# Four edits to the order of a one-core hybrid block: the S5 input's layout in DRAM, alternating layer-norm steps, the column-5 loads shared by up and down, and seven PSUM banks in the feed-forward

## The chip, the cores and the metric

One core of a Trainium2 chip runs the whole program. The metric is device microseconds of one execution; of the kernel before there are three runs, and their median is 1347.21 us (1343.9 to 1354.2). The engines are PE (matrix products), DVE (vector), ACT (activation), POOL (GpSimd) and SP (which issues nearly all the DMA loads of weights).

## What is computed

One layer on 256 latent and 256 context tokens of width 2048, batch 1. Cut to what matters here:

```python
m_lat = split(silu(c) @ w_ada + b_ada, 6)         # 2048 x 12288: six columns, each a vector of 2048
pl = split_in(modulate(x, m_lat[0], m_lat[1]) @ w_in)       # and pc, the same of ctx with m_ctx
ya = s5_mixer(pc[0], pl[0], ...)                  # 32 groups of 16 channels, 64 complex states, 2 directions
yd = mamba2_mixer(...)                            # bidirectional SSD
mix = concat([ya, chunk_gating(...), pool_mixer(...), yd]) @ w_out
h = layer_norm(ALPHA * x + m_lat[2] * mix, ln1_g, ln1_b)                      # "LN1" below
gate, val = split(modulate(h, m_lat[3], m_lat[4]) @ w_up, 2)                  # 2048 x 2*5632, "up"
f = (gelu(conv3x3(gate) + conv_b) * val) @ w_down                             # 5632 x 2048, "down"
out = layer_norm(ALPHA * h + m_lat[5] * f, ln2_g, ln2_b)                      # m_lat[5] is "column 5"
```

All weights are float32. Every large product is split into a high and a low part that the PE takes at a faster rate than float32.

## The kernel before, in words

Tokens lie along the free dimension (256 wide) and channels on the 128 partitions, so a vector of 2048 channels is 16 tiles (KT). A weight block of 128 x 1024 float32 (512 KB) is loaded by `load`, whose DMA stands on L158 and is issued by SP into one of a few buffers (`raw`, `pre`, `rxa`, `w`). `split` (L170 to L174) makes of each half of it a high part `wh` on ACT (L172) and a low part `wl` on DVE (L173), and `mm3` issues the matching pair of products on PE (L186 with `wh`, L187 with `wl`). DVE work outside this goes through the helpers `tt` (L202), `ts` (L197) and the scale-add on L205, so many different steps share these lines. A scheduler fixes the order of each engine's queue at build time from the order of the code, from priorities (`tc.high_priority`) and from dependencies; `yield` in the side work (a Python generator that `pump` advances between products) says how much PE time a piece stands for.

**Stages.** (1) 0 to 250 us: the six columns' products, interleaved with the input projection (`pA`, `bank`, L926). In it, four finished blocks of 128 S5 channels `pA[0..3]` are copied in time-reversed and straight form to `ut`, two buffers in turn, by two ACT copies each, and written to a DRAM tile `dU` (L968). The side work reads them back as `U` with 8 DMAs (L494), one for every eighth of the sequence, and makes from it 128 products `pS` in 8 steps (L503), each with `yield 3.4`; ACT copies them to `Z`, and a scan over `Z` follows on DVE (`wk<-Z,tab`, L202). (2) 250 to 438 us: the rest of the projection, the scan and the mixers, with products in between. (3) 438 to 565 us: the output projection `po`. (4) 565 to 596 us: LN1. `ln_stats` (L1137 to L1149) sums columns on PE, makes the mean, then the variance, its square root on ACT (L1147) and the reciprocal on DVE (L1148), and broadcasts both by products into two PSUM banks (L1149, `lsb`). Nine tiles or pairs then get `dT - mean` ("SU", L1217) and `dT * rstd` ("MU", L1218), both by `tt`, and ACT makes `hm` of each (L1220). The first two blocks of up (`NUP` = 2) are float32 products straight from `hm` and the raw weights, the two accumulators in turn (L1239). (5) 595 to 1091 us: up, 44 steps of `f`, each with two `half_up` (accumulator `pu`), a convolution on DVE and ACT (`cv`, `both`), and from `f` = 4 on one step of `gemv5`: one column-5 block of 512 KB loaded and accumulated on DVE (`acc<-raw,sc,acc`, 128 x 1024, L205), 32 blocks in all. (6) 1091 to 1338 us: down, 16 accumulators `pdn`, each with 44 K-tiles loaded in six blocks, and `ln_acc` after each. (7) the tail: `ln_stats` once more, SU and MU in pairs (L1350, L1351), scale and shift on ACT (L1340), store by SP (L1345).

**Banks.** PSUM tiles have tags: "main" with NMAIN = 3 banks and "side" with 4, the rest of the eight for `pg`. `pu`, `pdn`, `lst` (sums) and `lsb` take "main" in turn; `bank(name, tag)` may name another.

Of the kernel before, what the change touches and what calls it, by code (L numbers as in the profile page):

```python
# [51 lines left out]
def prep(i):  # L52
# [15 lines left out]
    wi = np.asarray(i["w_in"])[0]  # L68
    w1 = pm(np.concatenate([wi[:, :512], wi[:, 2560:2816]], 1))
    wt = pm(wi[:, :3584]).reshape(2, 8, P, 28, P).transpose(3, 0, 2, 1, 4).reshape(28, 2, P, 1024)  # L70
# [51 lines left out]
def build(tc, A, out, dbg=None):  # L122
# [41 lines left out]
    def wtile(n):  # L164
# [3 lines left out]
        return pool.tile([P, w], F32R, tag=tag, name="wh" if n == 0 else "wl", bufs=bufs)  # L168

    def split(src, n=512):  # L170
        h, l = wtile(0), wtile(1)
        S.copy(h[:, :n], src)  # L172
        V.tensor_sub(out=l[:, :n], in0=src, in1=h[:, :n])  # L173
        return h, l  # L174
# [141 lines left out]
    def side_gen():  # L316
# [175 lines left out]
        U = M.tile([P, G5, 64], F32, tag="U", name="U")  # L492
        for q in range(8):
            (GP, SY, (GP, SY)[q % 2])[BR].dma_start(out=U[q * 16:(q + 1) * 16], in_=G_["dU"].rearrange("(g h) q c -> h q g c", h=16)[:, q])  # L494

        Sth = [Z[:, n * 2048:n * 2048 + 2048].rearrange("p (c g k) -> p c g k", c=2, g=16) for n in range(2)]
        for e in range(8):
# [9 lines left out]
            for c_ in range(2):  # L507
                S.copy(St[hi, c_, g].rearrange("p g (s k) -> p g s k", s=2),
                       pv[hi, c_].rearrange("p g (s k) -> p g s k", s=2)[:, :, :, ::-1])
            yield 3.4  # L510

# [436 lines left out]
    for kp in range(8):  # L948
# [181 lines left out]
    def ln_stats(a12, s2_):  # L1130
# [11 lines left out]
        for n in range(4):  # L1142
            if n == 2:
                stt(st[:, 4:6], st[:, 0:2], -1.0, st[:, 0:2], MU, MU)
                tt(st[:, 4:6], st[:, 4:6], st[:, 2:4], AD)
                ts(st[:, 4:6], st[:, 4:6], 0.0, ALU.max)
                S.activation(out=st[:, 4:6], in_=st[:, 4:6], func=AF.Sqrt, bias=eps[:, 0:1])  # L1147
                V.reciprocal(out=st[:, 2:4], in_=st[:, 4:6])  # L1148
            PE.matmul(pb[n // 2][:, (n % 2) * P:(n % 2 + 1) * P], lhsT=st[:, n:n + 1].to_broadcast([P, P]), rhs=ident, start=True, stop=True)  # L1149
        return pb[0][:, :T], pb[1][:, :T]  # L1150

# [49 lines left out]
    for n in range(2):  # L1201
        rings[n][:] = [(wp, ("wh", "wl")[n], W_BUFS, 512), (fp, ("wh", "wl")[n], W_BUFS, 512)]
    mean, rstd = ln_stats(a12, s2l)
    gm = lnp.tile([P, 4, KT], F32, name="gm")
# [7 lines left out]
    hm = spare[0][:, 0:4096].rearrange("p (k t) -> p k t", k=KT)  # L1212
    raws += [spare[0][:, 4096:5120], spare[0][:, 5120:6144], spare[1][:, 0:1024], spare[1][:, 1024:2048]][:NSP]
    for c0, c1 in [(0, 1), (1, 2)] + [(ct, ct + 2) for ct in range(2, KT, 2)]:
        d = dT[:, c0:c1]
        bc = lambda a: a.unsqueeze(1).to_broadcast([P, c1 - c0, T])
        tt(d, d, bc(mean), SU)  # L1217
        tt(d, d, bc(rstd), MU)  # L1218
        for ct in range(c0, c1):
            S.activation(out=hm[:, ct], in_=dT[:, ct], func=AF.Identity, scale=gm[:, 0, ct:ct + 1],  # L1220
                         bias=gm[:, 1, ct:ct + 1])


# [51 lines left out]
    for f in range(FT):  # L1275
        if f >= G5S:
            next(g5, None)
# [28 lines left out]
        if FT - KT <= f:  # L1306
# [3 lines left out]
                             bias=gm[:, 3, ct:ct + 1]))  # L1310
    for _ in g5:
        pass


    b12 = lnp.tile([P, 2, T], F32, tag="a12", name="b12")
    shg = lnp.tile([P, T], F32, tag="shf", name="shg")
    for ct in range(KT):
# [11 lines left out]
        s2l = ln_acc(ct, pt, mm[:, 3], dT[:, ct], b12, shg)  # L1329
        if ct == 0:  # L1330
            sqrt_table()
    mean, rstd = ln_stats(b12, s2l)
    rm = fp.tile([P, 2, T], F32, tag="hm", name="rm", bufs=1)
# [69 lines left out]
```

## Time and profile before

| | us |
|---|---|
| median of 3 runs | 1347.21 (1343.9 to 1354.2) |
| the profiled execution | 1358.55 |
| span in the profile | 1356.7 |
| PE busy | 1292.0 (95% of the span) |
| DVE busy | 1002.4 (74%) |
| ACT busy | 628.8 (46%) |
| mean granted PE clock | 0.976 |

The span is the time between the first and the last instruction; the profiled execution's own time is 1.85 us more. Busy shares are means over stages with different limits. What counts is where PE stands still, what it waits for there, and where its granted clock falls.

### The profile page before, as it was taken

To read this page: it belongs to the slowest core of one execution; us is meant where nothing else is said; L and a number is where in the kernel's file an instruction comes from. 1 tells how busy PE (TensorE), PEld (TensorE's weight loads), DVE (VectorE), ACT (ScalarE), POOL (GpSimd) and SP (SyncE) were. 2 spreads that over 40 slices of the span, in tenths; PEclk is the share of its full clock that TensorE was granted. 3 is DMA by queue.
4 is the path that set the end of the run, shared out by engine and by line. 5 is a ranking of instruction groups with operands and counts; after the bars stand their busy time and mean duration, and the time that the engine had idled before them with its cause. 6 is when DMAs were issued, how large, how long until landed. Compare 5 with 4: busy or idle time off the path is not lost.

```text
span 1356.7 us, 23547 instructions
## 1 busy us (share of the span) xinstructions
PE 1292.0 (95%) x8680; PEld 1074.5 (79%) x8680; DVE 1002.4 (74%) x2144; ACT 628.8 (46%) x1234; POOL 31.5 (2%) x57
## 2 busy tenths in 40 slices
PE   5899999999899899899999999999999999999995
PEld 3788888666677577678888888887888888888884
DVE  8856419998465776678989898888998876655554
ACT  1233432344453444365555464555556654444443
POOL 0000100200200000000000000000000000000001
PEclk9899989999998999989999999999999999999997
DMA  9987665887862589757777667576765656666651
GB/s 356 389 312 252 242 153 193 293 288 259 279 217 76 209 313 332 289 179 225 230 225 232 219 221 238 175 227 210 244 203 186 187 170 196 186 188 197 181 171 62
DMA packets 88307, 305.36 MB, mean 225 GB/s; under 512 B 10376, under 2 KB 12568, under 8 KB 88064
## 3 DMA queue, kind: packets, MB, share of 16 engines
q1 hardware_dynamic: 85552, 295.58, 65.6%
q0 software_dynamic: 2640, 8.28, 2.4%
q8 instruction: 68, 1.11, 0.3%
q14 instruction: 47, 0.39, 0.1%
HBM read 298.02 MB, written 3.67 MB: 222 GB/s over the span
## 4 chain that ended last, share of the span: by engine, by line
PE 83%; DMA 6%; issue 5%; DVE 5%; ACT 1%; POOL 0%; SPq 0%; ACTq 0%; POOLq 0%; DVEq 0%
PE pu L186 23%; PE pu L187 12%; PE pdn L186 10%; PE pdn L187 5%; PE pA L926 5%; PE po L186 4%; PE pg L982 3%; PE bank L926 3%; DMA raw<-in_w 2%; PE bank L186 2%; PE pg L897 2%; PE po L187 2%; DMA raw<-in_wa 1%; PE pu L1239 1%; PE bank L187 1%
## 5 line engine op out<-in xcount | busy, mean ns | idle before, releaser
L173 DVE TENSOR_TENSOR wl<-raw,wh 128x512 fp32r<-128x512 f32 x616 | 420.0, 688 | 178.1 <-ACT wh L172 176.6
L172 ACT CAST wh<-raw 128x512 fp32r<-128x512 f32 x616 | 368.8, 619 | 342.9 <-PE pdn L186 103.9
L186 PE MATMUL pu<-XL,wh 128*128 128x512 f32 x1376 | 485.3, 396 | 1.9 <-DVE both L202 1.6
L187 PE MATMUL pu<-XL,wl 128*128 128x256 f32 x1376 | 387.4, 282 | 3.4 <-DVE wl L173 3.4
L186 PEld LDWEIGHTS pu<-XL,wh 128*128 128x128 f32 x1376 | 259.2, 188 | 63.8 <-PE pu L187 2.1
L187 PEld LDWEIGHTS pu<-XL,wl 128*128 128x128 f32 x1376 | 260.3, 189 | 4.5 <-DVE wl L173 4.5
L186 PE MATMUL pdn<-gR,wh 128*128 128x512 f32 x448 | 158.0, 395 | 0.0
L205 DVE SCALAR_TENSOR_TENSOR cv<-both,pc,cv 128x189 f32<-128x189 f32 (+2 forms) x344 | 146.9, 427 | 3.7 <-ACT cv L1289 1.3
L187 PE MATMUL pdn<-gR,wl 128*128 128x256 f32 x448 | 125.7, 281 | 0.0
L186 PEld LDWEIGHTS pdn<-gR,wh 128*128 128x128 f32 x448 | 84.1, 188 | 19.7
L187 PEld LDWEIGHTS pdn<-gR,wl 128*128 128x128 f32 x448 | 84.5, 189 | 0.0
L1299 ACT ACTIVATE cv<-cv 128x256 f32<-128x256 f32 x44 | 18.4, 418 | 134.8 <-DVE cv L205 134.7
L186 PE MATMUL po<-mxa,wh 128*128 128x512 f32 x192 | 71.8, 413 | 4.4 <-DVE mxa L615 4.4
L186 PE MATMUL pdn<-gxa,wh 128*128 128x512 f32 x192 | 67.9, 394 | 0.0
L186 PE MATMUL bank<-XL,wh 128*128 128x512 f32 x160 | 60.9, 417 | 0.0
L926 PE MATMUL pA<-XL,wh 128*128 128x256 f32 x192 | 55.0, 306 | 1.5 <-ACT XL L917 1.4
L187 PE MATMUL po<-mxa,wl 128*128 128x256 f32 x192 | 54.3, 283 | 0.0
L982 PE MATMUL pg<-raw,sc 128*32 128x512 f32 x384 | 52.8, 604 | 1.4 <-DMA raw<-in_wa 1.4
L186 PEld LDWEIGHTS po<-mxa,wh 128*128 128x128 f32 x192 | 36.8, 192 | 21.6 <-DVE mxa L615 5.7
L187 PE MATMUL pdn<-gxa,wl 128*128 128x256 f32 x192 | 53.8, 280 | 0.0
L205 DVE SCALAR_TENSOR_TENSOR acc<-raw,sc,acc 128x1024 f32<-128x1024 f32 x23 | 29.6, 1285 | 32.2 <-DMA raw<-in_wa 32.2
L187 PE MATMUL bank<-XL,wl 128*128 128x256 f32 x160 | 46.7, 292 | 1.9 <-DVE wl L173 1.9
(353 smaller groups left out, 2017.0 us busy)
## 6 DMA issues: line engine op xcount, KB each, us to landing
raw<-in_wa SPq DMA_DIRECT2D x165, 512.0 KB, 5.0
raw<-in_wu SPq DMA_DIRECT2D x147, 512.0 KB, 4.3
raw<-in_wd SPq DMA_DIRECT2D x80, 512.0 KB, 3.7
raw<-in_w SPq DMA_DIRECT2D x44, 512.0 KB, 5.4
raw<-in_wo SPq DMA_DIRECT2D x32, 512.0 KB, 5.6
rxa<-in_wu SPq DMA_DIRECT2D x29, 512.0 KB, 4.1
pre<-in_wa SPq DMA_DIRECT2D x20, 512.0 KB, 9.3
w<-in_w SPq DMA_DIRECT2D x16, 384.0 KB, 7.1
```

The costliest lines, as they stand in the source:

```text
L172: S.copy(h[:, :n], src)
L173: V.tensor_sub(out=l[:, :n], in0=src, in1=h[:, :n])
L186: chained(PE.matmul(pt.rearrange("p (n t) -> p n t", n=2), lhsT=wh, rhs=x, start=first, stop=False, skip_group_check=True))
L187: chained(PE.matmul(pt[:, :T], lhsT=wl, rhs=x[:, 0], start=False, stop=last, skip_group_check=True))
L205: V.scalar_tensor_tensor(out=o, in0=a, scalar=s, in1=b, op0=op0, op1=op1)
L897: chained(PE.matmul(pg[32 * j:32 * j + 32, 0:P], lhsT=sc[:, k], rhs=a[:, kk * 512 + j * P:kk * 512 + (j + 1) * P], start=(k == 0), stop=(k ...
L926: chained(PE.matmul(pt[:, s * T:(s + 1) * T], lhsT=w[:, c], rhs=x, start=(k == 0 and n == 0 and s == 0 and w is wh), stop=(k == KT - 1 and ...
L982: chained(PE.matmul(pg[32 * j:32 * j + 32], lhsT=sc[:, k], rhs=a[j // 2][:, (j % 2) * 512:(j % 2 + 1) * 512], start=(k == 0), stop=(k == K ...
L1239: chained(PE.matmul(ups[n][:, :T], lhsT=wr[n][:, kk * P:(kk + 1) * P], rhs=hm[:, k], start=(k == 0), stop=(k == KT - 1)))
L1299: S.activation(out=o, in_=o, func=AF.Gelu_apprx_tanh)
```

## The change

**Part 1, the S5 input.** The columns of the weight block that makes the S5 input are permuted on the host, from (group, channel) to (channel, group). `dU` becomes [8, 512, 64] instead of [512, 8, 64], so each of the four writes puts 8 pieces of 64 float32 per partition at different places in it, and the read of `U` is one DMA of 128 rows that are each 8 KB in a row. The copies and writes get high priority, and the second copy of each block goes to DVE. `yield` of the `pS` steps becomes 1.6.

**Part 2, alternating norms.** `behind` adds an order without a wait: SU of tile i stands behind MU of tile i-2 on DVE, and the first two SU behind the reciprocal, in LN1 and in the tail. In LN1 the weights' splits are held behind the scaling of tile 7 (HOLD = 8).

**Part 3, column 5.** Up takes a step of `gemv5` at every second `f` only, 17 in all; the other half's steps are in down, after four of the six blocks of an accumulator. `ln_acc` of the first accumulators waits (`waiting`) until column 5 is complete.

**Part 4, seven banks.** `pu` and `pdn` go over three "main" and four "side" banks in turn.

```diff
-    w1 = pm(np.concatenate([wi[:, :512], wi[:, 2560:2816]], 1))
+    w1 = pm(np.concatenate([wi[:, :512].reshape(D, G5, 16).transpose(0, 2, 1).reshape(D, 512), wi[:, 2560:2816]], 1))
...
+    held = [None, None]
     def split(src, n=512):
-        S.copy(h[:, :n], src)
-        V.tensor_sub(out=l[:, :n], in0=src, in1=h[:, :n])
+        behind(S.copy(h[:, :n], src), held[0])
+        behind(V.tensor_sub(out=l[:, :n], in0=src, in1=h[:, :n]), held[1])
...
+    def behind(made, first):
+        if first is not None:
+            tc.add_manual_dep(made.ins, first.ins.name,
+                              mybir.DependencyInfo(mybir.DependencyClass.NoSync, mybir.DependencyReason.DATA),
+                              reason="order on the engine")
+        return made
...
-        for q in range(8):
-            (GP, SY, (GP, SY)[q % 2])[BR].dma_start(out=U[q * 16:(q + 1) * 16], in_=G_["dU"].rearrange("(g h) q c -> h q g c", h=16)[:, q])
+        GP.dma_start(out=U.rearrange("p g c -> p (g c)"), in_=G_["dU"].rearrange("q (h g) c -> (q h) (g c)", h=16))
...
-            yield 3.4
+            yield 1.6
...
-    G_["dU"] = dr.tile([512, 8, 64], F32, name="dU")
+    G_["dU"] = dr.tile([8, 512, 64], F32, name="dU")
-    for n in range(4):
...
-        (S.copy if BC == 0 else V.tensor_copy)(u4[:, :, 1], src[:, :, 0])
-        (GP, SY)[BW].dma_start(out=G_["dU"][n * P:(n + 1) * P], in_=ut[:, n % 2].rearrange("p (q c) -> p q c", q=8))
+    with tc.high_priority(offset=FIRST):
+        for n in range(4):
...
+            S.copy(u4[:, :, 0], src[:, :, 1])
+            V.tensor_copy(out=u4[:, :, 1], in_=src[:, :, 0])
+            GP.dma_start(out=G_["dU"][:, n * P:(n + 1) * P].rearrange("q p c -> p q c"),
+                         in_=ut[:, n % 2].rearrange("p (q c) -> p q c", q=8))
...
+    muls = [inv, inv]
     for c0, c1 in [(0, 1), (1, 2)] + [(ct, ct + 2) for ct in range(2, KT, 2)]:
-        tt(d, d, bc(mean), SU)
-        tt(d, d, bc(rstd), MU)
+        behind(V.tensor_tensor(out=d, in0=d, in1=bc(mean), op=SU), muls[-2])
+        mul = V.tensor_tensor(out=d, in0=d, in1=bc(rstd), op=MU)
+        muls.append(mul)
...
+        if c1 == HOLD:
+            held[:] = [act, mul]
...
+    def turn(n):
+        return "main" if n % 7 < NMAIN else "side"
     def half_up(idx):
-        pt = bank(name="pu")
+        pt = bank("pu", turn(idx))
+        if idx > NUP:
+            held[:] = [None, None]
...
-        if f >= G5S:
+        if f >= G5S and f % 2 == 0 and f < G5S + 2 * (KT + 1):
             next(g5, None)
...
-        pt = bank(name="pdn")
-        if ct > 0:
-            tt(dT[:, ct], dT[:, ct], shg, SU)
+        pt = bank("pdn", turn(ct))
-        for s in range(0, FT, 8):
+        for n, s in enumerate(range(0, FT, 8)):
...
+            if n % 3 < 2 and g5 is not None and next(g5, g5) is g5:
+                g5 = None
+        waiting.append((ct, pt))
+        while g5 is None and waiting:
...
+            s2l = ln_acc(c_, p_, mm[:, 3], dT[:, c_], b12, shg)
...
+    muls = [inv, inv]
     for ct in range(0, KT - NGP, 2):
-        tt(d, d, b2(mean), SU)
-        tt(d, d, b2(rstd), MU)
+        behind(V.tensor_tensor(out=d, in0=d, in1=b2(mean), op=SU), muls[-2])
+        muls.append(V.tensor_tensor(out=d, in0=d, in1=b2(rstd), op=MU))
```

The line numbers below are each kernel's own (the new one's are 10 to 13 higher in the parts shown: L503 is L513, L926 is L936, L982 is L994).

On PE in the input projection, the place of the first `pS` products of the side work among the `bank` products, before:

```order
L926 MATMUL bank<-XL,wl 128x256
L926 MATMUL bank<-cxb,wl 128x256
L926 MATMUL bank<-XL,wh 128x256
L926 MATMUL bank<-cxb,wh 128x256
L926 MATMUL bank<-XL,wh 128x256
L926 MATMUL bank<-cxb,wh 128x256
L503 MATMUL pS<-U,mi 128x64 x32
L503 MATMUL pS<-U,half 128x64 x32
L926 MATMUL bank<-XL,wl 128x256
```

The same place in the changed kernel:

```order
L936 MATMUL bank<-XL,wl 128x256
L936 MATMUL bank<-cxa,wl 128x256
L994 MATMUL pg<-raw,sc 32x512 x3
L513 MATMUL pS<-U,mi 128x64 x32
L513 MATMUL pS<-U,half 128x64 x32
L994 MATMUL pg<-raw,sc 32x512
L936 MATMUL bank<-XL,wh 128x256
L936 MATMUL bank<-cxa,wh 128x256
L936 MATMUL bank<-XL,wh 128x256
L936 MATMUL bank<-cxa,wh 128x256
```

The `pS` products have moved up by 35 products, past the 34 `bank` products whose weights the PE waited for before, and into a run of `pg` products.

On DVE in LN1, from the steps before the first SU on. `lsb_5838` is the mean's bank and `lsb_5839` that of rstd; before:

```order
L197 TENSOR_SCALAR st_5836<-st_5836 128x2
L202 TENSOR_TENSOR dT_4685<-dT_4685,lsb_5838 128x256 x2
L202 TENSOR_TENSOR dT_4685<-dT_4685,lsb_5838 128x512 x3
L1148 RECIPROCAL st_5836<-st_5836 128x2
L202 TENSOR_TENSOR dT_4685<-dT_4685,lsb_5838 128x512 x4
L173 TENSOR_TENSOR wl_5968<-raw_5965,wh_5967 128x512
L173 TENSOR_TENSOR wl_5980<-raw_5965,wh_5979 128x512
L173 TENSOR_TENSOR wl_5994<-raw_5991,wh_5993 128x512
L202 TENSOR_TENSOR dT_4685<-dT_4685,lsb_5839 128x256 x2
L202 TENSOR_TENSOR dT_4685<-dT_4685,lsb_5839 128x512 x5
```

In the changed kernel the mean's bank is `lsb_5831` and that of rstd `lsb_5832`:

```order
L200 TENSOR_SCALAR st_5829<-st_5829 128x2
L1160 RECIPROCAL st_5829<-st_5829 128x2
L1230 TENSOR_TENSOR dT_4678<-dT_4678,lsb_5831 128x256 x2
L1231 TENSOR_TENSOR dT_4678<-dT_4678,lsb_5832 128x256 x2
L1230 TENSOR_TENSOR dT_4678<-dT_4678,lsb_5831 128x512 x2
L1231 TENSOR_TENSOR dT_4678<-dT_4678,lsb_5832 128x512
L1230 TENSOR_TENSOR dT_4678<-dT_4678,lsb_5831 128x512
L1231 TENSOR_TENSOR dT_4678<-dT_4678,lsb_5832 128x512
L1230 TENSOR_TENSOR dT_4678<-dT_4678,lsb_5831 128x512
L205 TENSOR_TENSOR XL_88<-rxa_5847,XL_88 128x512
L1231 TENSOR_TENSOR dT_4678<-dT_4678,lsb_5832 128x512
L1230 TENSOR_TENSOR dT_4678<-dT_4678,lsb_5831 128x512
```

Below this stand an MU, an SU, two `XL`, an MU, and then the ninth and last SU, which is the last reader of `lsb_5831`. The reciprocal has moved ahead of all the SU, the `wl` behind nearly all of it, and the last SU from the place before the first MU to the place behind seven of the nine MU and three `XL`.

On SP at the end of up and the start of down, before:

```order
L158 DMA raw<-in_wu 128x1024 x4
L158 DMA raw<-in_wa 128x1024
L158 DMA raw<-in_wu 128x1024 x32
L158 DMA raw<-in_wd 128x1024 x5
L158 DMA raw<-in_wd 128x512
L158 DMA raw<-in_wd 128x1024 x5
L158 DMA raw<-in_wd 128x512
```

In the changed kernel:

```order
L159 DMA raw<-in_wu 128x1024 x40
L159 DMA raw<-in_wd 128x1024
L159 DMA raw<-in_wa 128x1024
L159 DMA raw<-in_wd 128x1024
L159 DMA raw<-in_wa 128x1024
L159 DMA raw<-in_wd 128x1024 x2
L159 DMA raw<-in_wa 128x1024
L159 DMA raw<-in_wd 128x1024
L159 DMA raw<-in_wa 128x1024
L159 DMA raw<-in_wd 128x512
```

Sixteen column-5 loads now lie among the first 24 loads of down's weights, four to six of those, and as many fewer in up.

## Rows read from the trace of the kernel before

**Rows 1.** The page: busy us, share of the span and instructions of each engine.

```profile
PE 1292.0 (95%) x8680; PEld 1074.5 (79%) x8680; DVE 1002.4 (74%) x2144; ACT 628.8 (46%) x1234; POOL 31.5 (2%) x57
```

**Rows 2.** Chain of waits, 140 to 262 us: start us, us, what.

```profile
170.42 11.67 DMA raw<-in_w
...
182.79 6.97 PE bank L926 x34
...
206.72 5.94 PE bank L926 x48
```

**Rows 3.** DMA issues by kind: count, KB each, median us to landing.

```profile
raw<-in_wo SPq DMA_DIRECT2D x32, 512.0 KB, 5.6
...
pre<-in_wa SPq DMA_DIRECT2D x20, 512.0 KB, 9.3
...
dU<-Z POOLq DMA_DIRECT2D x4, 256.0 KB, 4.1
U<-dU POOLq DMA_DIRECT2D x8, 128.0 KB, 9.3
glu<-in_glu POOLq DMA_DIRECT2D x1, 1024.0 KB, 5.0
dY<-Z POOLq DMA_DIRECT2D x8, 64.0 KB, 2.9
```

**Rows 4.** Timeline of DVE and PE in LN1, 562 to 600 us.

```profile
571.05 2.54 DVE L202 TENSOR_TENSOR dT<-dT,lsb 128x256 f32<-128x256 f32 x5
573.51 0.16 DVE L1148 RECIPROCAL st<-st 128x2 f32<-128x2 f32 x1
...
577.77 3.74 DVE L202 TENSOR_TENSOR dT<-dT,lsb 128x256 f32<-128x256 f32 x7
...
573.81 1.19 PE L1149 MATMUL lsb<-cst,st 128*128 128x128 f32 x4 [2.81 <-DVE st L1148]
578.87 1.22 PE L1239 MATMUL pu<-rxa 128*128 128x256 f32 x2 [3.86 <-ACT rxa L1220]
579.88 1.06 PE L1239 MATMUL pu<-rxa,raw 128*128 128x256 f32 x2
```

**Rows 5.** Up, one window: us, busy (x) by engine, clock, DMA share, GB/s.

```profile
900.00:1000.00 100.00, 95.05 (x536) 81.74 (x535) 88.05 (x178) 52.68 (x114) 0.00 (x0) 1.00 0.71 226
```

**Rows 6.** What PE waited for, 596 to 1340 us.

```profile
PE pu L187 <- DVE wl L173: 3.4, 3, 2.4
PE pu L186 <- DVE both L202: 1.6, 2, 1.0
```

**Rows 7.** The page: column-5 steps: busy us, mean ns, idle before, releaser.

```profile
L205 DVE SCALAR_TENSOR_TENSOR acc<-raw,sc,acc 128x1024 f32<-128x1024 f32 x23 | 29.6, 1285 | 32.2 <-DMA raw<-in_wa 32.2
```

**Rows 8.** Timeline of the tail.

```profile
1342.75 7.26 DVE L202 TENSOR_TENSOR dT<-dT,lsb 128x512 f32<-128x512 f32 x12
...
1346.30 7.19 ACT L1340 ACTIVATE dT<-dT,pc 128x256 f32<-128x256 f32 x14 [1.89 <-POOL dT L1358]
```

**Rows 9.** Timeline of PE before the first `pS`, 176 to 184 us.

```profile
178.95 1.06 PE L982 MATMUL pg<-raw,sc 128*32 128x512 f32 x8
182.79 0.58 PE L926 MATMUL bank<-XL,wh 128*128 128x256 f32 x1 [2.77 <-ACT wh L172]
```

**Rows 10.** The window behind that wait, columns as above.

```profile
185.00:190.00 5.00, 5.00 (x31) 5.00 (x29) 0.94 (x2) 1.14 (x2) 0.00 (x0) 0.62 0.87 321
```

**Rows 11.** DVE's timeline at the scan's start: start us, us, engine, line, operation.

```profile
204.09 2.36 DVE L202 TENSOR_TENSOR wk<-Z,tab 128x1024 f32<-128x1024 f32 x2 [8.18 <-PE pS L503]
```

**Rows 12.** What PE waited for, 160 to 560 us: total, times, longest.

```profile
PE trb L677 <- ACT tab L661: 3.1, 1, 3.1
...
PE bank L187 <- DVE wl L173: 1.9, 1, 1.9
```

**Rows 13.** Timeline of DVE in LN1, the `XL` steps.

```profile
584.42 2.08 DVE L202 TENSOR_TENSOR XL<-rxa,XL 128x512 fp32r<-128x512 f32 x3
```

**Rows 14.** A window in the output projection.

```profile
540.00:560.00 20.00, 20.00 (x122) 14.22 (x115) 12.85 (x25) 8.65 (x16) 0.00 (x0) 1.00 0.92 338
```

More of the change, by code (lines that the diff above doesn't have):

```diff
@@ L960, in build @@
         ws = r
-    G_["dU"] = dr.tile([512, 8, 64], F32, name="dU")
+    G_["dU"] = dr.tile([8, 512, 64], F32, name="dU")
     ut = zs(2, (2, 512))
-    for n in range(4):
-        u4 = ut[:, n % 2].rearrange("p (q s c) -> p q s c", q=8, s=2)
-        src = pA[n].rearrange("p (s c q) -> p q s c", s=2, q=8)
-        S.copy(u4[:, :, 0], src[:, :, 1])
-        (S.copy if BC == 0 else V.tensor_copy)(u4[:, :, 1], src[:, :, 0])
-        (GP, SY)[BW].dma_start(out=G_["dU"][n * P:(n + 1) * P], in_=ut[:, n % 2].rearrange("p (q c) -> p q c", q=8))
+    with tc.high_priority(offset=FIRST):
+        for n in range(4):
+            u4 = ut[:, n % 2].rearrange("p (q s c) -> p q s c", q=8, s=2)
+            src = pA[n].rearrange("p (s c q) -> p q s c", s=2, q=8)
+            S.copy(u4[:, :, 0], src[:, :, 1])
+            V.tensor_copy(out=u4[:, :, 1], in_=src[:, :, 0])
+            GP.dma_start(out=G_["dU"][:, n * P:(n + 1) * P].rearrange("q p c -> p q c"),
+                         in_=ut[:, n % 2].rearrange("p (q c) -> p q c", q=8))
     ready.add("u")
@@ L1147, in ln_stats @@
                 S.activation(out=st[:, 4:6], in_=st[:, 4:6], func=AF.Sqrt, bias=eps[:, 0:1])
-                V.reciprocal(out=st[:, 2:4], in_=st[:, 4:6])
+                inv = V.reciprocal(out=st[:, 2:4], in_=st[:, 4:6])
             PE.matmul(pb[n // 2][:, (n % 2) * P:(n % 2 + 1) * P], lhsT=st[:, n:n + 1].to_broadcast([P, P]), rhs=ident, start=True, stop=True)
-        return pb[0][:, :T], pb[1][:, :T]
+        return pb[0][:, :T], pb[1][:, :T], inv
     def sqrt_table():
@@ L1202, in build @@
         rings[n][:] = [(wp, ("wh", "wl")[n], W_BUFS, 512), (fp, ("wh", "wl")[n], W_BUFS, 512)]
-    mean, rstd = ln_stats(a12, s2l)
+    mean, rstd, inv = ln_stats(a12, s2l)
     gm = lnp.tile([P, 4, KT], F32, name="gm")
@@ L1216, in build @@
         bc = lambda a: a.unsqueeze(1).to_broadcast([P, c1 - c0, T])
-        tt(d, d, bc(mean), SU)
-        tt(d, d, bc(rstd), MU)
+        behind(V.tensor_tensor(out=d, in0=d, in1=bc(mean), op=SU), muls[-2])
+        mul = V.tensor_tensor(out=d, in0=d, in1=bc(rstd), op=MU)
+        muls.append(mul)
         for ct in range(c0, c1):
-            S.activation(out=hm[:, ct], in_=dT[:, ct], func=AF.Identity, scale=gm[:, 0, ct:ct + 1],
+            act = S.activation(out=hm[:, ct], in_=dT[:, ct], func=AF.Identity, scale=gm[:, 0, ct:ct + 1],
                          bias=gm[:, 1, ct:ct + 1])
+        if c1 == HOLD:
+            held[:] = [act, mul]
     gR = fp.tile([P, 2, FT - KT, T], F32R, name="gR", bufs=1)
@@ L1310, in build @@
                              bias=gm[:, 3, ct:ct + 1]))
-    for _ in g5:
-        pass
     b12 = lnp.tile([P, 2, T], F32, tag="a12", name="b12")
     shg = lnp.tile([P, T], F32, tag="shf", name="shg")
+    s2l = None
+    waiting = []
     for ct in range(KT):
-        pt = bank(name="pdn")
-        if ct > 0:
-            tt(dT[:, ct], dT[:, ct], shg, SU)
+        pt = bank("pdn", turn(ct))
         k = 0
-        for s in range(0, FT, 8):
+        for n, s in enumerate(range(0, FT, 8)):
             m = min(8, FT - s)
@@ L1328, in build @@
                     k += 1
[L1329 to L1332, printed above, removed]
+            if n % 3 < 2 and g5 is not None and next(g5, g5) is g5:
+                g5 = None
+        waiting.append((ct, pt))
+        while g5 is None and waiting:
+            c_, p_ = waiting.pop(0)
+            if c_ > 0:
+                tt(dT[:, c_], dT[:, c_], shg, SU)
+            s2l = ln_acc(c_, p_, mm[:, 3], dT[:, c_], b12, shg)
+            if c_ == 0:
+                sqrt_table()
+    mean, rstd, inv = ln_stats(b12, s2l)
     rm = fp.tile([P, 2, T], F32, tag="hm", name="rm", bufs=1)
@@ L1384 @@
 NUP = 2
+HOLD = 8
 LAG = 4.0
```

## The prediction

> **What bounds the kernel now.** I read the busy shares first: PE is busy 1292.0 of 1356.7 us [rows 1], so 64.7 us at most lie in standstills, and an edit counts only if it removes one, adds one, or changes the granted clock. Four views then say which standstills the change touches. The chain of waits from 140 to 262 us shows the first: the chain goes through a weight load of 11.67 us ending at 182.09, and only then through `bank` L926 x34 [rows 2]. I put its length down to U's eight reads beside it, 4096 pieces of 256 bytes: 128 KB of them lands in 9.3 us, while 1 MB of `glu` lands in 5.0 [rows 3]. The second is LN1: DVE does nine subtractions of the mean (five of them ahead of the reciprocal), the `wl` of waiting weights, and then the scalings, while PE stands from the end of the rstd broadcast (573.81 + 1.19 = 575.0) to 578.87 [rows 4]. The third is up: one window of 100 us has PE at 95.05 [rows 5], and the waits name DVE, 3.4 and 1.6 us [rows 6], while DVE itself waits 32.2 us over 23 of the column-5 steps for their loads [rows 7]. The fourth is the tail, where 12 steps of DVE stand in a row ahead of most of ACT's 14 [rows 8].
>
> **The change part by part.** All sums are made against the profiled execution, 1358.55 us; the median of the runs shown is 1347.21, so its ratio to the profiled one is 0.9917, and the result is multiplied by that at the end. A measurement of this kernel tells about 1% (13.5 us) from no change.
>
> *Part 1, S5 input.* In the new order the first `pS` products stand where PE now stands still, ahead of the 34 `bank` products that wait. What the change gains there: PE stands 2.8 us, from the end of `pg` at 180.0 to 182.79 [rows 9], and the 34 products after it take 6.97 us instead of 34 x 5.94/48 = 4.2 [rows 2], because the clock granted after the standstill is 0.62 in the next window [rows 10]; together 5.6. The `pS` products stand behind the third of those eight `pg`, so PE comes to them at 178.95 + 3 x 1.06/8, about 179.4, and U must have landed by then. The first two writes go out at 154.7 and 155.5 as before; the third and fourth wait for the two `ut` buffers, so about 163. If they land in the 4.1 us of before, U's read starts at about 168, and 1 MB in whole rows, as `glu` at 5.0 [rows 3], gives 173 to 174; with two weight loads in front, 177. The margin is 2.4 us or more. The unknown is the write: its pieces are 256 bytes as the eight reads' are now. The nearest rows bound it: `dY` writes 64 KB in still smaller pieces and lands in 2.9, `dU` 256 KB at 4.1 and the read of 128 KB in small pieces at 9.3 [rows 3]. At the reads' price a pair of writes (512 KB, half of what the eight reads moved) takes about 9.3: pair one lands at 164.5, pair two near 175, U near 180.5, and PE loses about 1 us. I take `dY`'s price, since it is a write in small pieces: -5.6, with ends -7 (another 1.4 if `pS` needs no wait of its own) and +16.3 (rival A). The four copies moved to DVE cost nothing there: DVE stands idle for 8.18 us ahead of the scan [rows 11]. If that cover is gone, four copies at the 0.35 us of a 128x256 step [rows 4] delay `wl` by 1.4 us.
>
> By the Trainium skill (DMA: Bandwidth & Descriptors, section Specifications) transfers below 512 bytes pay a read-modify-write, and this speaks against the new 256-byte writes; rival A is what it would do here. The trace agrees for the small reads (9.3) and not for `dY` (2.9); by the rule alone, with each piece moved twice, the sum would be rival A's.
>
> *Middle.* With `pS` done about 10 us earlier (the stall plus 35 places), the scan on DVE starts by as much before 204.09 [rows 11]. PE itself comes 6 us earlier, so DVE has 4 us more lead. The waits that this may remove are 3.1 on ACT's `tab` and 1.9 on DVE's `wl` [rows 12]: 0 to -5.0. DVE's other work fills the same interval, so I take -2, less than half.
>
> *Part 2, LN1.* The reciprocal moves from 573.51 to about 571.4 (no subtraction ahead of it), the rstd bank is ready at about 572.9 instead of 575.0, and the first product can start near 574.6 instead of 578.87. That would be -4.2. But the two accumulators of the first blocks take the next main banks: there are three, `lst`, mean and rstd, so the second accumulator takes the mean's. Its first product waits for the last reader, the ninth subtraction. Before, this was over long ago; now 2 scalings of 128x256, 12 steps of 128x512 and 3 `XL` stand between rstd's arrival and its end. A 128x512 step costs 3.74 = 2 x 0.35 + 5 x 0.605 [rows 4], an `XL` about as much, three in 2.08 [rows 13]: 572.9 + 0.7 + 12 x 0.605 + 3 x 0.605 = 582.7. Before, PE was past its first two products and free of this wait at 579.88 [rows 4]. PE takes the products in order, so all that follow shift by some 2.9. The `wl` steps held back cost nothing, as the float32 products ahead of their use run for over 10 us. Ends: -4.2 (the wait does not bind) and +5 (`XL` waits for ACT). I take +2.9, since the order is fixed and only durations are estimated.
>
> *Part 2, tail.* Six subtractions, then six scalings take 7.26 us from 1342.75 [rows 8]. The rstd bank is ready at about 1344.0; alternating, the first scaling ends near 1344.6 instead of some 1347, and ACT may start 1.7 us before 1346.30. It then takes its 7.19 us and ends near 1352.3 instead of 1353.5, because DVE's last scaling comes where it did: -1.2 (ends -0.5 and -1.7).
>
> *Parts 3 and 4, up.* A step of column 5 occupies DVE for 1.285 us, and the 23 that were not in the `rxa` buffers made it stand 32.2 us, 1.4 each [rows 7], while the `wl` behind it in the queue waits too, and PE for that. With a step in every second `f`, DVE has one step of 1.285 less in two `f`, and 17 of the 32 waits are left in up, each with a load issued earlier in the buffers' turn. The waits on `wl` go (3.4), and the standstill of the window at 900 us, 4.95 [rows 5], is the same by another view. Seven banks let PE run ahead of `both`, 1.6 us [rows 6]. I take -5.0, all of it; ends 0 and -5.0.
>
> *Parts 3 and 4, down.* The 16 loads of column 5 now lie among the first 24 loads of down, so 36 blocks of 0.524 MB, 18.9 MB (20 of down's, halves counted as halves, and 16 of column 5), must come while PE works through 20 blocks of down, each 8 K-tiles of 0.35 us, 56 us: 337 GB/s. The output projection already moves 338 GB/s in one window with PE at 20.00 of 20 [rows 14], so the rate itself is not out of reach. Five buffers in turn must each come round in 7.0 us, and with the split blocks held in reserve (eight halves, 11 us over eight turns) in 8.4. The output projection's loads, at that rate, landed in 5.6 [rows 3]; some 2 us of splitting are added: 7.6, under 8.4. I take 0; ends 0 and +23 (rival B).
>
> The sum: -5.6 - 2 + 2.9 - 1.2 - 5.0 + 0 = -10.9, so 1347.65 by the profiled execution, and 1347.65 x 0.9917 = 1336.5.
>
> **The rivals.**
>
> *A, the small writes are slow.* If each piece costs twice a read's, a pair of writes takes 18.6 instead of 9.3 [rows 3]: pair one lands at 173.7, pair two, which needs the same two buffers, near 193.3, and U near 198.5. PE takes `pS` in its order and stands 19.1 us from 179.4 on, 16.3 more than the 2.8 of before, the lower clock behind it stays, and the lead of the scan is gone. The sum becomes -10.9 + 5.6 + 2 + 16.3 = +13.0, and 1371.55 x 0.9917 = 1360.2, slower by 1.0%. The change is slower than before from the point where U lands after 185.5 (there PE's added stand is the 3.3 us that the rest of the sum gains). For it: the reads' 9.3. Against it: `dY` at 2.9, and `glu`'s 5.0 for the new read. Chance 0.06.
>
> *B, down starves.* Where loads come in behind others they landed in 9.3 (`pre`) [rows 3]. With 9.3 + 2 = 11.3 per turn against 8.4, eight turns lose 23 us: 1347.65 + 23 = 1370.65, or 1359.3, slower by 0.9%. For it: DVE has its waits on `in_wa` already in up. Against it: 338 GB/s with PE full [rows 14]. A landing of 6.9 in its place gives 8 x 0.5 = +4, or 1340. Chance 0.10.
>
> *C, the wait for the mean's bank does not bind.* Then LN1 gives -4.2, 7.1 less than the sum: 1340.55, or 1329. For it: the three main banks come in turn by a count that I read from the order, and ACT or PE rows do not show banks. Against it: the names in the order. Chance 0.10.
>
> *D, the lead pays in full, or the clock stays up.* The two waits of the middle go entirely and U's stretch gives 7: 4.4 less, 1343.25 and 1332. Chance 0.15.
>
> *E, the waits in up move rather than go.* A standstill before one product becomes one before the next, as DVE still works at 88.05 of 100 [rows 5]: up gives 0, middle 0, the sum is -3.9, or 1343. Chance 0.21.
>
> **How the numbers follow.** The forecast, with all terms within some 3 us of what I took, has 0.38: 1336.5. A to E have 0.62. Faster by over 1% is below 1333.7: C (0.10), most of D (0.12) and the lower part of the forecast (0.17), 0.39. Slower by over 1% is above 1360.7: the dearer half of A and of B, with little to spare, 0.06. The rest, 0.55, is within 1%. The range reaches from 1326 (C and D together, 1325) to 1350 (half of B's price, or a little over half of A's); the upper half of both, 0.09, is left out above, and a gain beyond C and D, 0.08, below.
>
> **What would show it.** *U:* `pS` x64 starting near 179.4 directly behind `pg`, one U read of about 5 us, no granted clock of 0.62 at 185; wrong if PE waits for U there. *Middle:* the scan starting near 194 and the rows `tab` 3.1 and `wl` 1.9 smaller. *LN1:* the reciprocal near 571.4 less the shift, one product, then a wait of PE on a DVE subtraction of 7 us or so. *Up:* no window under 99 of 100, column-5 waits at half their number. *Down:* windows of PE at 100 in the 60 us after up; wrong if PE waits on `wl` or `wh` behind `raw<-in_wd` or `raw<-in_wa`. *Tail:* ACT's scaling starting 2.2 us after the rstd broadcast. The forecast as a whole is wrong if the time is over 1350 or under 1326.

## The result

The changed kernel takes 1358.57 us (median of 10 runs, 1355.67 to 1361.26) against 1348.21 for the kernel before (10 runs, 1343.9 to 1357.52). The ratio of the runs is 1.0052 (95% interval 1.0026 to 1.0077): slower by half a per cent, where 1336.5 with a range of 1326 to 1350 was forecast. (The two medians by themselves lie 0.77% apart; the ratio is what all later runs are compared by.) Its profiled execution takes 1357.17 us, span 1355.4, near its own median. That of before took 1358.55, ten above its median, so the two traces set side by side show a difference of -1.4 us only. Which part of the older trace is usual has to be settled first (the first experiment, and the one with seven banks alone).

Stage by stage, from the start of a stage's first product (or of the last `po`) in each trace, the changed kernel stands against before at: first `pS` -9.7, first `pdt` -4.4, last `po` -3.9, first `half_up` -0.9, first `pdn` -10.1, last `pdn` -0.4, end -1.4. So LN1 costs 3.1, up gains 9.2, down costs 9.7, and the tail gains 1.0.

**U's stretch.** PE's timeline, 178 to 196 us, answers to [rows 9]:

```profile
178.89 1.06 PE L994 MATMUL pg<-raw,sc 128*32 128x512 f32 x6
179.88 7.36 PE L513 MATMUL pS<-U,mi 128*128 128x64 f32 x64
```

The window behind it answers to [rows 10] (busy by engine, granted clock, DMA share, GB/s), and DMA by kind to [rows 3]:

```profile
185.00:190.00 5.00, 5.00 (x48) 5.00 (x46) 0.00 (x0) 3.44 (x10) 0.00 (x0) 1.00 0.32 105
...
dU<-Z POOLq DMA_DIRECT2D x4, 256.0 KB, 5.0
U<-dU POOLq DMA_DIRECT2D x1, 1024.0 KB, 5.7
```

There is no standstill ahead of `pS`, the clock is 1.00 where it was 0.62, and the 256-byte writes land in 5.0 against 4.1 of the 2 KB pieces before.

**LN1.** The timelines of DVE and PE, 564 to 596 us, answer to [rows 4]:

```profile
567.39 0.17 DVE L1160 RECIPROCAL st<-st 128x2 f32<-128x2 f32 x1 [0.36 <-ACT st L1159]
...
577.97 0.69 DVE L1230 TENSOR_TENSOR dT<-dT,lsb 128x512 f32<-128x512 f32 x1
...
570.04 1.22 PE L1256 MATMUL pu<-rxa 128*128 128x256 f32 x2 [1.15 <-ACT rxa L1234]
578.77 1.19 PE L1256 MATMUL pu<-rxa,raw 128*128 128x256 f32 x2 [7.50 <-issue]
```

The first product is 8.8 us earlier than in [rows 4], and then PE stands 7.5 us. "issue" says that the trace shows nothing it waited for. The ninth subtraction (L1230) ends at 578.66 and PE goes on 0.11 later.

**Up and down.** The window of [rows 5] has no standstill any more:

```profile
900.00:1000.00 100.00, 100.00 (x583) 87.40 (x582) 84.53 (x175) 60.93 (x122) 0.00 (x0) 0.98 0.63 197
```

What PE waited for, 560 to 1340 us (total, times, longest), answers to [rows 6], with a new row in place of `wl` and `both`:

```profile
PE pu L1256 <- issue: 7.5, 1, 7.5
PE pdn L189 <- DVE gxb L205: 5.2, 1, 5.2
...
```

DVE's timeline ahead of it, 1055 to 1103 us, and PE's row:

```profile
1081.38 0.42 DVE L205 TENSOR_TENSOR gxb<-cv,gxb 128x256 fp32r<-128x256 f32 x1
1081.93 1.29 DVE L208 SCALAR_TENSOR_TENSOR acc<-raw,sc,acc 128x1024 f32<-128x1024 f32 x1
...
1087.56 1.28 DVE L208 SCALAR_TENSOR_TENSOR acc<-raw,sc,acc 128x1024 f32<-128x1024 f32 x1 [0.62 <-DMA raw<-in_wa]
...
1091.79 1.28 DVE L208 SCALAR_TENSOR_TENSOR acc<-raw,sc,acc 128x1024 f32<-128x1024 f32 x1 [0.95 <-DMA raw<-in_wa]
...
1097.04 1.28 DVE L208 SCALAR_TENSOR_TENSOR acc<-raw,sc,acc 128x1024 f32<-128x1024 f32 x1 [0.58 <-DMA raw<-in_wa]
...
1099.92 1.28 DVE L208 SCALAR_TENSOR_TENSOR acc<-raw,sc,acc 128x1024 f32<-128x1024 f32 x1
1101.13 0.42 DVE L205 TENSOR_TENSOR gxb<-cv,gxb 128x256 fp32r<-128x256 f32 x1
...
1101.60 0.80 PE L189 MATMUL pdn<-gxb,wh 128*128 128x512 f32 x1 [5.17 <-DVE gxb L205]
```

`gxb` at 1101.13 is the last gate tile, which the end of down's first accumulator needs. Between it and the `gxb` before stand five column-5 steps: 5 x 1.28 us and waits of 0.62, 0.95 and 0.58 for their loads, 8.6 together. The two `gxb` are 19.8 us apart; in the kernel before they were 10.9 (1087.31 and 1098.20). There the last `gxb` came 7 us after down's first product (1098.20 against 1091.25); here 20 us after it (1101.13 against 1081.19). In the 5 us window behind the standstill the granted clock is 0.50, the lower of its two levels (columns as above):

```profile
1100.00:1105.00 5.00, 3.40 (x11) 2.92 (x12) 2.69 (x4) 0.83 (x2) 0.00 (x0) 0.50 0.82 254
```

**Tail.** ACT's scaling starts at 1344.79 instead of 1346.30 [rows 8]:

```profile
1344.79 7.22 ACT L1370 ACTIVATE dT<-dT,pc 128x256 f32<-128x256 f32 x14 [0.76 <-DVE dT L1382]
```

### The profile page after: what moved, and what is told of

It is laid out like the page before. It is cut to its first block, busy times and chain, and to the rows that moved or that the text cites. A ratio compares the mean times of both kernels' runs of the same rounds, so it can differ in the third digit from the quotient of the medians.

```text
span 1355.4 us, 23455 instructions
## 1 busy us (share of the span) xinstructions
PE 1291.2 (95%) x8680; PEld 1072.5 (79%) x8680; DVE 1009.4 (74%) x2148; ACT 644.5 (48%) x1230; POOL 28.5 (2%) x50
## 4 chain that ended last, share of the span: by engine, by line
PE 74%; DVE 3%; DMA 3%; ACT 1%; issue 1%; ACTq 0%; DVEq 0%
PE pu L189 24%; PE pu L190 12%; PE pdn L189 12%; PE pdn L190 6%; PE po L189 4%; PE pg L994 2%; PE po L190 2%; PE bank L189 2%; DMA raw<-in_w 1%; PE pu L1256 1%; PE bank L190 1%; PE bank L1095 1%; PE bank L1096 1%; PE bank L1097 1%; DVE wl L176 1%
## 5 line engine op out<-in xcount | busy, mean ns | idle before, releaser
L175 ACT CAST wh<-raw 128x512 fp32r<-128x512 f32 x614 | 377.1, 621 | 432.3 <-PE pu L189 131.8
L190 PE MATMUL pdn<-gR,wl 128*128 128x256 f32 x448 | 126.5, 282 | 0.0
L936 PE MATMUL pA<-XL,wh 128*128 128x256 f32 x192 | 55.3, 308 | 1.4 <-ACT XL L927 1.4
L208 DVE SCALAR_TENSOR_TENSOR acc<-raw,sc,acc 128x1024 f32<-128x1024 f32 x27 | 34.7, 1285 | 28.9 <-DMA raw<-in_wa 28.7
L994 PE MATMUL pg<-raw,sc 128*32 128x512 f32 x384 | 55.1, 604 | 0.3 <-DMA raw<-in_wa 0.2
L175 ACT CAST wh<-rxa 128x512 fp32r<-128x512 f32 x58 | 35.9, 623 | 35.9 <-PE pu L189 24.3
L189 PEld LDWEIGHTS po<-mxa,wh 128*128 128x128 f32 x192 | 36.0, 188 | 19.8 <-DVE mxa L625 4.2
```

Of the source, the lines that this page charges most:

```text
L175: behind(S.copy(h[:, :n], src), held[0])
L189: chained(PE.matmul(pt.rearrange("p (n t) -> p n t", n=2), lhsT=wh, rhs=x, start=first, stop=False, skip_group_check=True))
L190: chained(PE.matmul(pt[:, :T], lhsT=wl, rhs=x[:, 0], start=False, stop=last, skip_group_check=True))
L208: V.scalar_tensor_tensor(out=o, in0=a, scalar=s, in1=b, op0=op0, op1=op1)
L936: chained(PE.matmul(pt[:, s * T:(s + 1) * T], lhsT=w[:, c], rhs=x, start=(k == 0 and n == 0 and s == 0 and w is wh), stop=(k == KT - 1 and ...
L994: chained(PE.matmul(pg[32 * j:32 * j + 32], lhsT=sc[:, k], rhs=a[j // 2][:, (j % 2) * 512:(j % 2 + 1) * 512], start=(k == 0), stop=(k == K ...
```

## The experiments

Every ratio is against runs of the kernel before on the same chip, 95% interval in brackets. The changed kernel stands at 1.0052 by the same measure. Product times named without a row are starts read from each trace like the stages above.

### The kernel before once more

No edit.

> The kernel before, unchanged, for a second profile of it. The profiled execution of before took 1358.55 us, its median is 1348.2: something like 10 us of its standstills do not belong to a usual execution. Theory 1 (the standstill of up is an accident): in this profile up, from the first half_up to the first pdn, takes about 487 us instead of 495.8, and U's stretch is as it was (pS near 189.6). Theory 2 (U's stretch is the accident): up takes about 495 us and pS comes near 184 or earlier. The ratio should be 1.000.

Measured: 0.9994 [0.9969, 1.002], 1352.15 us median; its runs go from 1344.8 to 1359.9. The profiled execution, 1357.28, is again one of the long ones. What PE waited for in U's stretch and in up, and the window of up:

```profile
PE bank L926 <- ACT wh L172: 6.0, 1, 6.0
...
PE pu L186 <- DVE both L202: 1.8, 3, 0.8
PE pu L187 <- DVE wl L173: 1.2, 2, 0.8
...
900.00:1000.00 100.00, 96.85 (x544) 83.08 (x543) 89.43 (x182) 53.17 (x116) 0.00 (x0) 1.00 0.72 229
```

Neither theory as put: both places have standstills here too, 6.0 instead of 2.8 for U and 3.0 instead of 5.0 in up, and up takes 492.6 us instead of 495.8. They vary from execution to execution, and that a run of before may take 1344 or 1360 fits this, though no short run of before itself was traced. The longer runs also have a lower mean clock: of the runs of before beside this one, the shortest third has 0.981 on average and the longest third 0.977. How much of their length is the clock and how much the waits is not shown.

### Column 5 wholly in up

```diff
-        if f >= G5S and f % 2 == 0 and f < G5S + 2 * (KT + 1):
+        if f >= G5S:
...
+    for _ in g5:
+        pass
+    g5 = None
     b12 = lnp.tile([P, 2, T], F32, tag="a12", name="b12")
```

> The changed kernel, with column 5 taken wholly in up again (a step in every f from 4 on, none in down). Theory 1, the column-5 steps ahead of the last gate steps in DVE's queue cost the 5.3 us of standstill at 1096 us and some 3 us of lower clock behind it: 8 to 10 us less than the changed kernel, about 1349, with no PE standstill at the start of down, and up again at or below 490 us because seven banks are still there. Rival: the steps taken out of up paid for themselves, and with them back up stands still for 5 us or more: within 3 us of the changed kernel.

Measured: 0.9977 [0.9956, 0.9998], 0.75% under the changed kernel, 10 us. The standstill is gone, and up takes 488.8 us with all its 32 loads, with no standstill at 900 to 1000. The changed kernel's up takes 486.6, and nearly the whole difference of 2.2 lies in one place: the 32 small products that reduce one half of `acc` on PE take 2.03 us in either kernel, once in up and once in down in the changed one, twice in up here.

### Down's steps one accumulator later

```diff
-            if n % 3 < 2 and g5 is not None and next(g5, g5) is g5:
+            if ct >= 1 and n % 3 < 2 and g5 is not None and next(g5, g5) is g5:
```

> The changed kernel, with the steps of column 5 in down beginning at the second accumulator instead of the first, so that none of them is near the last gate steps; there are as many loads in down as in the changed kernel. Theory 1 (order in DVE's queue): the standstill at the start of down goes, 8 us less, about 1350. Rival (rate of the loads in down): the standstill moves by one accumulator, to about 1112, and the time stays within 2 us of 1358.6.

Measured: 1.0002 [0.9979, 1.0025], 0.5% under the changed kernel (about 7 us). PE waits 0.7 us in all on `pdn`. The standstill does not move to the next accumulator, so the rate of the loads is not what it was for.

### The column-5 steps behind the last gate

The sharper form: loads and steps stay where they are, only DVE's order changes.

```diff
+        sub = V.tensor_tensor(out=gT(1, f), in0=o, in1=gT(0, f), op=SU)
+        if f == FT - 1:
+            gate[0] = sub
...
-                    stt(acc, a, sc[:, k, 0:1], acc, MU, AD)
+                    behind(V.scalar_tensor_tensor(out=acc, in0=a, scalar=sc[:, k, 0:1], in1=acc, op0=MU, op1=AD), gate[0])
```

(The first step of `acc` likewise.)

> The changed kernel with one order added on DVE: the column-5 steps of down stand behind the last gate subtraction (gxb). Loads, their places in SP's queue and the number of steps are those of the changed kernel. Theory 1 (DVE's order): the PE wait for gxb of 5.2 us and the lower clock behind it go, 6 to 9 us less than the changed kernel, ratio 0.998 to 1.001. Rival (the loads' rate at the start of down): the standstill stays, on wl or wh or the loads, as the held-back steps keep their buffers longer: ratio 1.004 or more.

Measured: 0.9989 [0.9966, 1.0011], 0.63% under the changed kernel, 8.5 us. The last `gxb` now comes 5.6 us after down's first product (1089.51 against 1083.91) instead of 20. The waits of PE from 1080 us on name no `pdn` at all, and the two windows there are full, with DMA at 354 GB/s in the second:

```profile
1080.00:1100.00 20.00, 20.00 (x116) 17.49 (x115) 16.43 (x28) 8.43 (x16) 0.00 (x0) 1.00 0.70 225
1100.00:1120.00 20.00, 20.00 (x116) 17.49 (x115) 17.39 (x22) 8.96 (x16) 0.00 (x0) 1.00 0.97 354
```

Down takes 249.2 us from first to last `pdn`, against 247.0 with column 5 in up, which is the reduction of `acc` again, and 256.7 in the changed kernel. With the same loads and another order on DVE the loss is gone: the loads were not the limit.

### The first accumulators of up in side banks

```diff
-    ups = [bank(name="pu") for _ in range(NUP)]
+    ups = [bank("pu", "side") for _ in range(NUP)]
```

> The changed kernel, with the first two accumulators of up in the side banks instead of the main ones, so that neither takes the mean's bank. Theory 1 (LN1's wait of 7.5 us after the first product is for the mean's last reader): the wait goes, LN1 from the last po to the first half_up takes about 26 us instead of 33.4, 7 us less in all, about 1351.5. Rival (PE waits there for hm or the clock, whatever the bank): less than 2 us.

Measured: 0.9992 [0.9971, 1.0013], 0.6% under the changed kernel, 8 us. From the last `po` to the first `half_up` is 26.0 us instead of 33.4. PE's timeline has the second group right behind the first:

```profile
571.55 1.22 PE L1256 MATMUL pu<-rxa 128*128 128x256 f32 x2 [1.15 <-ACT rxa L1234]
572.56 1.06 PE L1256 MATMUL pu<-rxa,raw 128*128 128x256 f32 x2
```

So the wait that the trace calls "issue" was for the bank that held the mean. Part of the gain is lost again in this version's down, which takes 259.4 us instead of 256.7: PE comes to the last gate tile earlier and waits longer for it.

```profile
PE pdn L189 <- DVE gxb L205: 7.2, 1, 7.2
```

### Both mends together

The edits of column 5 wholly in up and of the side banks.

> Both of the edits before together on the changed kernel: column 5 wholly in up, and the first two accumulators of up in side banks. Theory 1 (the two losses are independent waits of PE): 0.0075 for the one and 0.0060 for the other come off 1.0052, ratio 0.992, about 11 us faster than the kernel before. Rival (the first products then wait for hm or for weights instead, or up starts earlier and only waits more for column-5 loads): 0.996 or more.

Measured: 0.9916 [0.9901, 0.9931], median 1341.83, 1341.3 to 1342.27 in 4 runs. The two gains add up, though so exactly by luck: with the side banks alone some 2.7 us were lost again in down, and the intervals leave room for several us. The version lies 0.84% under the kernel before, and none of the study is measurably faster. Its four runs lie closer together than those of before.

### The S5 input's part undone

On that version, the writes, the eight reads, the copies, the column order and `yield 3.4` of before:

```diff
-        GP.dma_start(out=U.rearrange("p g c -> p (g c)"), in_=G_["dU"].rearrange("q (h g) c -> (q h) (g c)", h=16))
+        for q in range(8):
+            (GP, SY, (GP, SY)[q % 2])[BR].dma_start(out=U[q * 16:(q + 1) * 16], in_=G_["dU"].rearrange("(g h) q c -> h q g c", h=16)[:, q])
```

> The run before (column 5 in up, side banks) with the S5 input's part undone: the four writes and eight reads of before, all copies on ACT, yield 3.4. Theory 1 (part 1 removes the stall of 2.8 to 6.1 us before the bank products and the lower clock behind it): 4 to 6 us slower than the run before, ratio 0.995 to 0.997, with the stall back near 180 us. Rival (the stall is an accident of two profiled executions, or its gain is lost to the waits behind it up to the output projection): within 1.5 us of the run before.

Measured: 0.9916 [0.9901, 0.9931], median 1341.81 against 1341.83: part 1 is worth nothing that can be measured. Three marks from each trace show where its gain goes. With the old way, the wait before the `bank` products (shorter here than in the two traces of before), the first `po`, the last `po`, and two waits:

```profile
182.80 0.39 PE L937 MATMUL bank<-XL,wh 128*128 128x256 f32 x1 [1.45 <-ACT wh L175]
...
436.21 0.59 PE L189 MATMUL po<-mxa,wh 128*128 128x512 f32 x1
...
561.02 0.28 PE L190 MATMUL po<-mxa,wl 128*128 128x256 f32 x1
...
PE po L189 <- DVE mxa L626: 4.0, 4, 1.8
...
PE pl L872 <- ACT vals L870: 0.6, 2, 0.5
```

With the new way:

```profile
434.33 0.59 PE L189 MATMUL po<-mxa,wh 128*128 128x512 f32 x1
...
561.97 0.28 PE L190 MATMUL po<-mxa,wl 128*128 128x256 f32 x1
...
PE po L189 <- DVE mxa L625: 2.2, 4, 0.9
PE pl L871 <- ACT vals L869: 2.2, 2, 2.1
...
PE pdt L1070 <- ACT dts L1068: 1.2, 1, 1.2
```

With the new way PE comes to `po` 1.9 us earlier and leaves it 0.95 us later. A wait of `pdt` and a longer one of `pl` have come in; they are in all ten traces with the new way (`pdt` 0.9 to 2.5, `pl` 2.2 to 2.4) and in none of the four with the old way (`pl` 0.6 to 0.7, no row for `pdt`). Shorter waits on `mxa` pay for part of them. The rest of the loss lies in the first quarter of the products of `po`, which take 46.2 us instead of 43.4; in this trace the granted clock is 0.91 from 450 to 470 us. The other traces tell order and clock apart. Where the clock is 1.00 throughout, `po` takes 124.8 and 125.0 us with the old way (this run, and the kernel before with seven banks) and 126.3 to 126.8 in four traces with the new one; where it falls, 126.5 and 126.8 with the old way and 127.6 to 128.2 with the new. So the new order costs `po` some 1.3 to 2 us, and the clock as much again in some executions.

### Three banks

On the fastest version, `turn` gives "main" always:

```diff
-        return "main" if n % 7 < NMAIN else "side"
+        return "main"
```

> The run with column 5 in up and side banks for the first two accumulators, but pu and pdn after those on the three main banks alone. Theory 1 (seven banks take away the waits on both and half the waits on wl in up, as PE may run on while an accumulator is read): 3 to 6 us slower, with PE waits named pu on DVE both or wl in up. Rival (the waits in up are for column-5 loads and do not depend on banks): within 1.5 us.

Measured: 0.9954 [0.9937, 0.9972], 0.38% (5 us) slower than with seven. Waits in up and the window:

```profile
PE pu L189 <- DVE both L205: 3.3, 4, 1.0
...
PE pu L190 <- DVE wl L176: 0.8, 1, 0.8
...
900.00:1000.00 100.00, 96.78 (x548) 83.37 (x546) 89.92 (x184) 55.20 (x120) 0.00 (x0) 1.00 0.71 225
```

With seven banks neither row is there.

### Seven banks alone, on the kernel before

```diff
-        pt = bank(name="pu")
+        pt = bank("pu", turn(idx))
...
-        pt = bank(name="pdn")
+        pt = bank("pdn", turn(ct))
```

> The kernel before with seven banks for pu and pdn, and nothing else. Theory 1 (banks are what part 3 and 4 gain in up): up loses its standstills of 3 to 6 us, ratio 0.996 as between the runs with three and seven banks. Rival (banks only help together with the other edits): 0.999 or more.

Measured: 0.997 [0.9944, 0.9997]; `both` is gone from the waits in up and `wl` is at 0.8. Part 4 alone makes the kernel before faster, by 0.3%, with an interval that only just excludes no change; up takes 491.8 us.

This trace also shows what a usual execution is like ahead of LN1. Up to the end of `po` PE, DVE and ACT run the same instructions in the same order as in the kernel before, and the profiled execution, 1349.66, is near its median of 1349.09. There is no wait at `bank` L926 in it, the clock behind is 1.00 instead of the 0.62 of [rows 10], and `pS` comes 4.8 us earlier than in the trace of before, as does the last `po` (560.41 against 565.17):

```profile
184.82 7.33 PE L503 MATMUL pS<-U,mi 128*128 128x64 f32 x64 [0.98 <-DMA U<-dU]
...
185.00:190.00 5.00, 5.00 (x47) 5.00 (x46) 0.62 (x2) 1.27 (x3) 0.00 (x0) 1.00 0.78 307
```

Against this execution the changed kernel is 4.9 us ahead at `pS` and 0.8 behind at the last `po` (561.23).

### LN1 in the scheduler's order

On the fastest version, without the order of part 2 in LN1:

```diff
-        behind(V.tensor_tensor(out=d, in0=d, in1=bc(mean), op=SU), muls[-2])
+        V.tensor_tensor(out=d, in0=d, in1=bc(mean), op=SU)
...
-        if c1 == HOLD:
-            held[:] = [act, mul]
```

> The run with column 5 in up and side banks for the first two accumulators, with LN1's subtractions and scalings in the scheduler's own order again and no weights held back (the tail still alternates). Theory 1 (alternating lets the first product start some 4 us earlier and hides the rest behind products): 4 to 5 us slower than that run, ratio 0.995. Rival (PE then waits for later hm instead): within 1.5 us.

Measured: 0.9988 [0.9966, 1.0009], 0.7% above the version with alternation; by the trace 5.3 us of it are LN1 (30.8 us from the last `po` to the first `half_up` against 25.5), the size that was expected. Another 1.8 lie in up (490.5 against 488.7), which the run does not explain; the rest, some 2.5, is within the two intervals. Both standstills of [rows 4] are back:

```profile
570.74 1.19 PE L1161 MATMUL lsb<-cst,st 128*128 128x128 f32 x4 [4.00 <-DVE st L1160]
575.80 1.22 PE L1254 MATMUL pu<-rxa 128*128 128x256 f32 x2 [3.88 <-ACT rxa L1234]
```

### Sharing with both mends, in two ways

Down's steps one accumulator later, with side banks:

> Column 5 shared, its steps in down beginning at the second accumulator, and the first two accumulators of up in side banks. Theory 1 (sharing costs down about 2.5 us by its loads and gives up nothing once the banks are there): about 3 us slower than with column 5 in up, ratio 0.995. Rival (sharing helps up by the 3 us that its standstills are shorter): equal or faster than with column 5 in up, 0.992 or less.

Measured: 0.9971 [0.9952, 0.9991], slower by 0.55% than with column 5 in up. In the profiled execution, 3.4 us above its median, 5 us of the distance arise before LN1, where the two kernels do the same, and 2.3 in down beyond the 2.15 of the reduction; its window 1160 to 1180 has a clock of 0.91. Then the steps behind the last gate, with side banks:

> The changed kernel with both mends: the column-5 steps of down behind the last gate subtraction, and the first two accumulators of up in side banks. It differs from the run with column 5 wholly in up (0.9916) only by sharing the column. Theory 1 (once the order is mended, sharing neither gains nor loses): ratio 0.991 to 0.994. Rival (sharing itself costs through its loads in down): 0.996 or more. A gain by sharing would show as 0.989 or less.

Measured: 0.9942 [0.9916, 0.9968], span 1340.2 against 1340.4 of the fastest version, whose interval this one overlaps; the ratio is just above the 0.994 that was expected. Once the order is mended, sharing brings no gain that these runs show.

## Why the prediction was wrong

**The ratio and the terms counted one thing twice.** The sum was made against an execution of 1358.55, multiplied by 0.9917 for the median. That factor already takes away 11 us, part of which the trace has as standstills that other executions lack or have shorter; the same standstills, in U's stretch and in up, were then counted as gains. The second trace of before shows them at other sizes (6.0 and 3.0 us), and the run with seven banks alone, near its median, is 4.8 us ahead of the trace of before when `po` ends, with the same order of work. The rest of the 11 us is not traced. The forecast needed the terms at their usual size, or no factor.

**Down, term 0, was the step that failed most.** It asked whether the loads come fast enough, and that part was right: 337 GB/s was the estimate, 354 was moved with PE full in the run that changes DVE's order, and nothing starved. The step named no engine order. The column-5 steps stand in DVE's queue ahead of the last gate subtraction, and the end of the first accumulator waits for that. What is queued behind a waiting instruction, and who waits for that, was worked out for LN1 and not here. Rival B had the right side and stage with the wrong mechanism (loads landing in 9.3, 23 us): it is 5.2 us of standstill, the lower clock behind it, about 8.5 by the run that changes DVE's order alone.

**U and the middle, -5.6 and -2.** All steps up to `pS` came as worked out: PE at `pS` at 179.88 for 179.4, U's read landing 5.7 after its issue, clock 1.00 at 185, the scan at 194.48 for 194. Rival A did not occur. Two steps failed. The 5.6 was read from one long execution: in the one near its median, with the same eight reads under way, there is no wait for `bank` and no low clock behind it, and `pS` waits 1.3 us. And what is gained at `pS`, 4.9 us against that execution, is not kept: waits at `pdt` and `pl` come in, `po` takes some 1.3 to 2 us longer in the new order, and the `tab` and `wl` waits of [rows 12] stay (3.2 and 2.2 in the changed kernel for 3.1 and 1.9). The run with part 1 undone is equal. The lead of the scan gained nothing.

**LN1, +2.9.** Right: 3.1 by the traces (582.7 less 579.88 is 2.8, not 2.9). The wait for the mean's bank ended 4.0 us before the 582.7 that was worked out, as PE came to LN1 3.9 us earlier. The run with side banks shows its whole price, 7.3 us in its trace, and what alternation gives when the bank does not bind: about 5. Rival C had that side; the bank did bind.

**Up, -5.0.** Right in sum and wrong in its source. Seven banks give 0.3 to 0.4% (two runs); taking half the column-5 steps out of up gives nothing beside them (of the 17 steps left in up 16 load a block, and the last is the reduction). The change's 9.2 us against the trace of before holds 2.15 of reduction that moved to down. DVE's waits for column-5 loads hardly fell (28.7 us over 24 steps, for 32.2 over 23): half of them moved.

**Tail, -1.2.** Right: -1.0.

With the measured terms the sum for the median is 0 for U and the middle, +3 for LN1, -4 to -5 for up, -1 for the tail and +8.5 for down: +5.5 to +6.5, or 0.4 to 0.5%, against the ratio's 0.52%. By the two medians it is 10.4 us; the rest of that is not explained by these terms.

## What to carry to other kernels

In these runs work that waits for a transfer, put at a stage's border because the engine has room there on average, delayed the last short steps that the next stage needs, because it stood ahead of them in the engine's order. Read the order around the border, not the rate of the loads. Before a median is worked out from a profiled execution, compare the two; where the execution is long, its standstills may be partly its own, and a second trace, best of an execution near the median, tells which. And when an order is changed so that a buffer's readers end later, list what takes that buffer next, and give it another if one is free.

## What the runs showed of the hardware

A wait of 7.5 us for a PSUM bank whose readers on DVE were not done appears in the trace as "issue", as if PE waited for nothing; the last reader's end, 0.11 us before PE goes on, was the only sign, until other banks took the wait away. Writes of 256 KB in 256-byte pieces landed in 4.8 to 5.2 us (medians of the ten traces with the new way), some 0.8 above the 4.1 to 4.3 of 2 KB pieces (four traces), while reads of 128 KB in 256-byte pieces, eight under way together, took 8.9 to 11.0 in those four.
